# Output projection of a hybrid decoder layer: the second product of twelve pairs computed from HGRN2's half of y, among the attention's rest, with its sums kept in DRAM

## The chip, the cores and the metric

The kernel runs on one core of a Trainium2 chip. The metric is the device time of one execution in microseconds (us); the median of several runs is compared. The engines are TensorE (PE; its weight loads are listed apart as PEld), VectorE (DVE), ScalarE (ACT), GpSimd (POOL) and SyncE (SP), which issues every DMA of this kernel, in the order of its instructions. Each engine works through its own list in order, and waits where an instruction's operand isn't there yet.

## What is computed

The reference is one decoder layer over 4096 rows of width 1024, in float32. Cut to what matters:

```python
hn = _rmsnorm(x, mix_norm_w[layer])
proj = hn @ w_in[layer]                       # 1024 -> 4096 columns
...
y_attn = _head_rmsnorm(attn, ...) * silu(ag)  # 8 heads of 64, three dilated windows
y_hgrn = _head_rmsnorm(rec, ...) * silu(hg)   # 4 heads of 128, gated linear recurrence
mixed = jnp.concatenate([y_attn, y_hgrn], axis=-1)
x = x + mixed @ w_out[layer]
return _rmsnorm(x, final_norm_w)
```

The left half of `mixed` (512 columns) comes from the attention, the right half from the recurrence HGRN2. The kernel calls the two together `y` and keeps them in DRAM (`y_d`, 4096 x 1024).

## The kernel before, in words

**Stages.** First the attention's columns of the input projection, by 16 pairs of 128-row blocks. Then HGRN2's columns and its recurrence, head by head and pair by pair (`hgrn_pair`, L340), and beside it the attention: a generator, `attention()` (L624), from which `take` (L631) draws pieces between the pieces of HGRN2. When HGRN2's last pair is written, a part of the attention's eighth head is left, and `take(10 ** 9)` (L874) writes it all out: this is the attention's rest. Last comes the output projection with the residual and the final norm.

**The attention's rest.** It is the last part of head 7 at dilation 1: scores (`score`, L423/L424 on PE, L434 on DVE, L436 on ACT), transposes of the weights (`flip`, L446, with L449 on ACT and L450 on DVE), products with V (`weigh`, L458, whose V tiles `vh` are loaded at L531), and the sum of their two halves (`o`, L464 on ACT and L568 on DVE). After every eight blocks `finish` (L581) joins the three dilations: transposes (L603, L604), multiplications into the tile `pr` (L606 on DVE; the tile has one buffer), sums and norm on POOL (L609 to L618), and the store of 1024 rows of y (L619). There are four such stores for head 7. `summed_wo` (L968) is laid among it: it loads w_out (L974, four buffers `xr`), builds sums of its blocks on DVE (L982 to L989) and splits them (L858 on ACT, L859 on DVE).

**The output projection.** It is done by 16 pairs of row blocks, as a 2 x 2 by 2 x 2 block product with seven products in place of eight. Of a pair's y, `A11` is the attention's half of the first block, `A12` HGRN2's half of the first block, `A21` and `A22` the same of the second block; `B11` to `B22` are the 512 x 512 blocks of w_out, and S1 to S4 and T1 to T4 are sums of them. A product of 128 x 512 by 512 x 512 is called a half (`half`, L719): every operand is split into a rounded part (hi) and the rest (lo), and for each of four slices of 128 it takes three matmuls, hi·hi, hi·lo and lo·hi (L723, L724, L725), twelve in all. The first output block's left half is A11·B11 + A12·B21: `begin` (L919) does A11·B11 into a PSUM bank, copies it to `u2` (L927), does S4·B22 in between, adds A12·B21 into the first bank (L930) and adds the bank to the residual `xr` (L931). This A12·B21 is the pair's second product.

`load_y` (L876) loads the four quarters of a pair's y (L882, tile `vh`, three buffers), transposes each on PE in four pieces (L886) and makes the splits and sums on ACT, DVE and POOL (L170/L171, L893/L894, L901 to L909). `finish_pair` (L939) does the five other products, and `final_norm` (L958) the norm and the store. For each pair the loads of the next one are written ahead of its `finish_pair`.

**What sets the order.** The program is written in the order above, and a scheduler with its own model of the times then lays each engine's list. It moves instructions past one another where their operands allow it. Buffers limit it: tiles `raw` have three buffers, PSUM `proj` two, `hp1` and `po` one each, `att` four.

Of the kernel before, what the change touches and what calls it, by code (L numbers as in the profile page):

```python
# [49 lines left out]
def layer(ctx: ExitStack, tc: tile.TileContext, x, xT, xP, pos, w_in, w_out, nw, anw, hnw, lbraw, fnw,  # L50
# [7 lines left out]
    qk_d = [dram.tile([128, 4, S], F32, name=f"qk_d{p}") for p in range(4)]  # L58
    v_d = [dram.tile([S, 2, 128], F32, name=f"v_d{p}") for p in range(4)]
    xh_d = [dram.tile([4, 128, 1024], F32, name=f"xh_d{t}") for t in range(NB // 2)]  # L60
    sg_d = dram.tile([S, 512], F32, name="sg_d")
    y_d = dram.tile([S, D], F32, name="y_d")
    ml_d = dram.tile([NH, 2, 2, S], F32, name="ml_d")
# [655 lines left out]
    def half(ps, X, W, start=True):  # L719
        for k in range(4):  # L720
            c = slice(k * 128, (k + 1) * 128)
            (hi, lo), (whi, wlo) = X, W[k]
            T.matmul(ps, hi[:, c], whi, start=start and k == 0, stop=False, skip_group_check=not start)  # L723
            T.matmul(ps, hi[:, c], wlo, start=False, stop=False, skip_group_check=not start)  # L724
            T.matmul(ps, lo[:, c], whi, start=False, stop=(k == 3), skip_group_check=not start)  # L725
# [147 lines left out]
    dma(fnwt, fnw.partition_broadcast(128))  # L873
    take(10 ** 9)  # L874

    def load_y(t):  # L876

        a, X = {}, {}
# [9 lines left out]
        def split(name, src, eng, tags=None):  # L888
            if tags is None:
                X[name] = parts(split_tile(src, eng, xp, "xs", 5))  # L890
                return
            hi, lo = (tp.tile([128, 512], F32R, name=n, bufs=b) for n, b in tags)
            A.activation(hi, src, AF.Copy)  # L893
            eng.tensor_tensor(lo, src, hi.bitcast(F32), op=ALU.subtract)  # L894
            X[name] = hi, lo
# [6 lines left out]
        s2 = tp.tile([128, 512], F32, name="pot", bufs=2)  # L902
        V.tensor_tensor(s2, s1, a[0, 0], op=ALU.subtract)
        split("S2", s2, G, (("pt", 5), ("pt", 5)))
        split("A12", a[0, 1], V)
        split("S1", s1, G)
        V.tensor_tensor(a21, a[0, 0], a21, op=ALU.subtract)
        split("S3", a21, G, (("pt", 5), ("pt", 5)))
# [10 lines left out]
    def begin(t, X, third=True):  # L919

        xr = [fp.tile([128, D], F32, name="xr", bufs=4) for _ in range(2)]
        for i in range(2):
            dma(xr[i], x[(2 * t + i) * 128 : (2 * t + i + 1) * 128, :])
        pa = bank()
        half(pa, X["A11"], WO["B11"])
        u2 = fp.tile([128, 512], F32, name="u2", bufs=2)
        A.activation(u2, pa, AF.Copy)  # L927
        if third:
            third_product(X, xr)
        half(pa, X["A12"], WO["B21"], start=False)  # L930
        V.tensor_tensor(xr[0][:, c0], pa, xr[0][:, c0], op=ALU.add)  # L931
        return xr, u2

# [122 lines left out]
```

## Time and profile before

| | |
|---|---|
| median of 3 runs | 2739.09 us (2737.37 to 2740.02) |
| the profiled execution's own time | 2743.28 us |
| its span, first to last instruction | 2741.5 us |
| PE matmul busy | 2553.6 us (93%) |
| DVE busy | 2024.1 us (74%) |
| ACT busy | 1747.1 us (64%) |
| POOL busy | 1069.4 us (39%) |
| mean granted TensorE clock | 0.963 |

How to read it: times count from the span's start. A line such as `2507.41 0.39 PE L723 MATMUL att<-whi,xs ... x1` is the start, the duration, the engine, the line of the kernel, the operation, the tile written and the tiles read; a bracket behind it gives the idle time of the engine just before, and what ended it. In rows with groups, `x15 | 10.3, 687 | 4.8` means fifteen instructions, 10.3 us in all, 687 ns each, and 4.8 us of idle time ahead of them. Matmuls overlap, so that the time of a row of them is read from the difference of their starts. A wait reads: engine and line, what released it, us in total, times, the longest. PEclk is the share of full speed that TensorE's clock was granted.

### The profile page before, as it was taken

What the parts mean: (1) busy time and instruction counts of PE and PEld (TensorE: products, weight loads), DVE (VectorE), ACT (ScalarE), POOL (GpSimd) and SP (SyncE); (2) the same over time, 40 slices, a digit from 0 to 9 for tenths busy, and PEclk for the clock granted to TensorE, in tenths of its full rate; (3) what the DMA queues carried; (4) which work ended last, traced back from release to release, by engine and by line L of the source; (5) the groups of instructions that cost most, each with busy time, mean ns of one, the idle gap of its engine ahead of it and who ended that gap; (6) DMA issues with size and microseconds to landing.
All of it is one profiled execution on the core that took longest, in us unless ns stands there. A gap on an engine that the chain in (4) does not pass through costs nothing.

```text
span 2741.5 us, 51929 instructions
## 1 busy us (share of the span) xinstructions
PE 2553.6 (93%) x17138; PEld 2308.2 (84%) x17138; DVE 2024.1 (74%) x5310; ACT 1747.1 (64%) x4811; POOL 1069.4 (39%) x1012
## 2 busy tenths in 40 slices
PE   5899989999979999899999899999999998599998
PEld 4678867888879989799999799999899997488886
DVE  8787788777637788787787787776776877756665
ACT  7755565555548768768677678577686687434443
POOL 5455646665434464132231231331331421244443
PEclk8999999999979999999999899999999999699999
DMA  6854463444686775674874755855855743445453
GB/s 229 252 183 138 150 206 118 145 147 144 191 257 185 236 233 184 198 192 129 214 195 130 214 168 151 224 160 155 245 148 162 213 144 116 137 119 157 144 153 108
DMA packets 452192, 477.99 MB, mean 174 GB/s; under 512 B 119336, under 2 KB 334420, under 8 KB 451924
## 3 DMA queue, kind: packets, MB, share of 16 engines
q1 hardware_dynamic: 451924, 474.68, 58.6%
q8 instruction: 137, 2.24, 0.3%
q14 instruction: 131, 1.07, 0.1%
HBM read 348.16 MB, written 126.37 MB: 173 GB/s over the span
## 4 chain that ended last, share of the span: by engine, by line
PE 69%; DMA 10%; DVE 10%; ACT 4%; issue 3%; POOL 2%; SPq 1%; POOLq 0%; DVEq 0%; ACTq 0%
PE proj L199 19%; PE po L458 6%; PE m L725 6%; PE m L723 6%; PE m L724 6%; PE att L446 4%; PE att L723 3%; PE att L724 3%; PE att L725 3%; PE att L423 3%; PE att L424 3%; DMA y_d<-pr 1%; DMA raw<-x 1%; DVE pr L606 1%; DMA raw<-w_in 1%
## 5 line engine op out<-in xcount | busy, mean ns | idle before, releaser
L199 PE MATMUL proj<-xs,whi 128*128 128x256 f32 x2048 | 429.0, 294 | 21.6 <-ACT whi L161 12.1
L199 PE MATMUL proj<-whi,xs 128*128 128x256 f32 x2048 | 431.7, 293 | 4.2 <-DVE hz L306 4.2
L199 PEld LDWEIGHTS proj<-xs,whi 128*128 128x128 f32 x2048 | 331.2, 193 | 27.9 <-ACT whi L161 13.7
L199 PEld LDWEIGHTS proj<-whi,xs 128*128 128x128 f32 x2048 | 335.1, 193 | 5.9 <-DVE hz L306 4.5
L434 DVE CUSTOM_DVE_ANT_0 pt<-att,mask 128x256 f32<-128x256 f32 (+1 forms) x768 | 269.4, 388 | 75.8 <-PE att L424 73.7
L199 PE MATMUL proj<-xs,wlo 128*128 128x256 f32 x1024 | 300.5, 293 | 0.9 <-DVE wlo L162 0.9
L199 PE MATMUL proj<-wlo,xs 128*128 128x256 f32 x1024 | 300.0, 293 | 0.0
L450 DVE TENSOR_TENSOR pl<-att,ph 128x512 fp32r<-128x512 f32 (+1 forms) x384 | 237.7, 626 | 58.5 <-ACT ph L449 55.8
L436 ACT ACTIVATE pt<-pt,ml 128x256 f32<-128x256 f32 (+1 forms) x512 | 238.1, 467 | 55.3 <-DVE ml L434 54.2
L446 PE MATMUL att<-ident,pt 128*128 128x128 f32 x1368 | 228.3, 280 | 6.8 <-ACT pt L436 4.7
L449 ACT ACTIVATE ph<-att 128x512 fp32r<-128x512 f32 (+1 forms) x384 | 203.4, 542 | 47.4 <-PE po L458 28.6
L458 PE MATMUL po<-ph,vh 128*128 128x128 f32 (+1 forms) x856 | 212.4, 278 | 14.5 <-issue 10.1
L458 PE MATMUL po<-pl,vh 128*128 128x128 f32 (+1 forms) x856 | 207.3, 288 | 3.5 <-DVE pl L450 3.5
L199 PEld LDWEIGHTS proj<-xs,wlo 128*128 128x128 f32 x1024 | 197.3, 193 | 2.8 <-DVE wlo L162 1.3
L199 PEld LDWEIGHTS proj<-wlo,xs 128*128 128x128 f32 x1024 | 198.0, 193 | 1.2 <-issue 1.0
L458 PEld LDWEIGHTS po<-ph,vh 128*128 128x128 f32 x856 | 166.8, 195 | 19.4 <-issue 12.8
L446 PEld LDWEIGHTS att<-ident,pt 128*128 128x128 f32 x1368 | 162.3, 144 | 12.2 <-ACT pt L436 6.5
L458 PEld LDWEIGHTS po<-pl,vh 128*128 128x128 f32 x856 | 167.4, 196 | 5.2 <-DVE pl L450 4.7
L464 ACT ACTIVATE pot<-po 64x512 f32<-64x512 f32 (+1 forms) x256 | 124.4, 486 | 73.9 <-DVE o L568 37.9
L723 PE MATMUL m<-tw,ss 128*128 128x512 f32 x384 | 154.9, 404 | 15.2 <-ACT tw L170 7.4
L724 PE MATMUL m<-tw,ss 128*128 128x512 f32 x384 | 154.5, 402 | 4.1 <-DVE tw L171 4.1
L725 PE MATMUL m<-tw,ss 128*128 128x512 f32 x384 | 155.7, 406 | 0.0
(304 smaller groups left out, 7695.0 us busy)
## 6 DMA issues: line engine op xcount, KB each, us to landing
xs<-xh_d SPq DMA_DIRECT2D x192, 512.0 KB
xr<-xT SPq DMA_DIRECT2D x128, 256.0 KB
qk_d<-stk SPq DMA_DIRECT2D x128, 256.0 KB
xh_d<-xs SPq DMA_DIRECT2D x64, 512.0 KB
vh<-v_d SPq DMA_DIRECT2D x512, 64.0 KB
raw<-x SPq DMA_DIRECT2D x64, 256.0 KB
v_d<-hl SPq DMA_DIRECT2D x128, 128.0 KB
raw<-xP SPq DMA_DIRECT2D x64, 256.0 KB
```

Source lines behind the costliest of these rows:

```text
L199: m = T.matmul(o, l, r, start=first is None, stop=(k == KT - 1 and g == len(groups) - 1 and n == 2))
L423: T.matmul(o, q[:, j % 2 * 128 : (j % 2 + 1) * 128], cols(KH, *ks), start=True, stop=False)
L434: V.tensor_tensor_reduce(out=p_, in0=o, in1=mask[:, (1, 4, 16).index(d), 256 - 128 * nk : 256], scale=-0.125, scalar=3e38, op0=ALU.add, op ...
L436: A.activation(p_, p_, AF.Exp, scale=-1.0, bias=m, accum_out=l)
L446: T.transpose(ps[:, n * 128 : (n + 1) * 128], loc[u], ident)
L449: A.activation(ph[:, :w], ps[:, :w], AF.Copy)
L450: V.tensor_sub(pl[:, :w], ps[:, :w], ph[:, :w].bitcast(F32))
L458: T.matmul(po[:, 128 * c : 128 * (c + n)], v, rh, start=(s == 0), stop=(s == len(steps) - 1))
L464: A.activation(t[o : o + 64, c], po[64 - o : 128 - o, c], AF.Copy)
L723: T.matmul(ps, hi[:, c], whi, start=start and k == 0, stop=False, skip_group_check=not start)
L724: T.matmul(ps, hi[:, c], wlo, start=False, stop=False, skip_group_check=not start)
L725: T.matmul(ps, lo[:, c], whi, start=False, stop=(k == 3), skip_group_check=not start)
```

## The change

For the pairs 0 to 11 (`AHEAD = 12`) the second product is taken out of `begin` and computed earlier, in a loop of its own that is written behind `take(10 ** 9)` and ahead of the first `load_y`. For each such pair the loop loads HGRN2's half of the first block (`y_d[..., 512:1024]`, into a `raw` tile), transposes it on PE into `hp1`, splits it (hi on ACT, lo on DVE, into an `xs` tile), does the half with B21 into a `proj` bank, loads the left half of the same rows of x into another `raw` tile, adds the bank to it on DVE and stores the sum in DRAM (`p2_d[t]`, 256 KB).

In the output projection these pairs no longer split A12 and no longer do A12·B21. The residual tile of the first block is loaded in two parts, the stored sum for the left half and x for the right. All else of a pair is as before: the four loads and sixteen transposes of its y stay, since S4 needs A12 too. The pairs 12 to 15 are unchanged.

```diff
+    AHEAD = 12
+    p2_d = [dram.tile([128, 512], F32, name=f"p2_d{t}") for t in range(AHEAD)]
...
     take(10 ** 9)
 
+    for t in range(AHEAD):
+
+        yt = xp.tile([128, 512], F32, name="raw", bufs=3)
+        dma(yt, y_d[2 * t * 128 : (2 * t + 1) * 128, 512:1024])
+        pt_ = ps_h.tile([128, 512], F32, name="hp1")
+        for k in range(4):
+            c = slice(k * 128, (k + 1) * 128)
+            T.transpose(pt_[:, c], yt[:, c], ident)
+        a12 = parts(split_tile(pt_, V, xp, "xs", 5))
+        po2 = ps_p.tile([128, 512], F32, name="proj")
+        half(po2, a12, WO["B21"])
+        xt = xp.tile([128, 512], F32, name="raw", bufs=3)
+        dma(xt, x[2 * t * 128 : (2 * t + 1) * 128, 0:512])
+        V.tensor_tensor(xt, po2, xt, op=ALU.add)
+        dma(p2_d[t], xt)
...
-        split("A12", a[0, 1], V)
+        if t >= AHEAD:
+            split("A12", a[0, 1], V)
...
-            dma(xr[i], x[(2 * t + i) * 128 : (2 * t + i + 1) * 128, :])
+            rows = slice((2 * t + i) * 128, (2 * t + i + 1) * 128)
+            if i or t >= AHEAD:
+                dma(xr[i], x[rows, :])
+            else:
+                dma(xr[i][:, c0], p2_d[t])
+                dma(xr[i][:, c1], x[rows, c1])
...
-        half(pa, X["A12"], WO["B21"], start=False)
+        if t >= AHEAD:
+            half(pa, X["A12"], WO["B21"], start=False)
```

The scheduler lays the loop's instructions among those of the attention's rest; the lists that follow are its orders, before and in the changed kernel. The changed kernel's lines lie 2 further down to the loop, 18 further down in `load_y` and 25 further down from the end of `begin` on.

On DVE, ahead of head 7's second finish (the multiplications into `pr` that close each list), there stood before the sums of w_out's blocks (`xr`, `u2`), a piece of the norm (`nrr`) and the sum `o1`:

```order
L141 TENSOR_TENSOR nrr_29316<-nrr_29316,nrq_29319 128x8
L568 TENSOR_TENSOR o1_29516<-po_29563,pot_29577 64x256
L989 TENSOR_TENSOR xr_31984<-xr_31984,u2_31992 128x512
L982 TENSOR_TENSOR xr_32004<-xr_32004 128x512
L984 TENSOR_TENSOR u2_32013<-xr_32005,xr_32004 128x512
L987 TENSOR_TENSOR xr_32004<-xr_32005,xr_32004 128x512
L989 TENSOR_TENSOR xr_32005<-xr_32005,u2_32013 128x512
L606 TENSOR_TENSOR pr_29619<-att_29620,wt_29611 128x2x192
```

In the changed kernel the same place has adds of the new loop (L891, `proj` and x's `raw`) and a lo part (L173, from `hp1`):

```order
L142 TENSOR_SCALAR nrq_29331<-nrq_29331 128x8
L570 TENSOR_TENSOR o1_29528<-po_29575,pot_29586 64x256
L143 TENSOR_TENSOR nrr_29328<-nrr_29328,nrq_29331 128x8
L570 TENSOR_TENSOR o1_29528<-po_29575,pot_29589 64x256
L891 TENSOR_TENSOR raw_32035<-proj_32022,raw_32035 128x512
L173 TENSOR_TENSOR xs_32046<-hp1_32041,xs_32046 128x512
L891 TENSOR_TENSOR raw_32062<-proj_32049,raw_32062 128x512
L608 TENSOR_TENSOR pr_29631<-att_29632,wt_29623 128x2x192
```

The sums of w_out's blocks stand a little further up, and the adds of the turns 3 and 4 now stand directly ahead of the finish. By the twelfth turn, twelve such lo parts and eleven adds stand ahead of the first multiplication of the fourth finish.

On SP, before, the stretch from the last early load of w_out over finish's first and second store (`y_d` from `pr`), with the gate's load (`sgt`) and V's loads (`vh`):

```order
L974 DMA xr_32005<-w_out 128x1024
L531 DMA vh_29863<-v_d3_67 128x4x128
L619 DMA y_d_85<-pr_29287 128x8x64
L585 DMA sgt_29607<-sg_d_84 128x8x64
L531 DMA vh_29972<-v_d3_67 128x4x128
L531 DMA vh_30055<-v_d3_67 128x4x128
L619 DMA y_d_85<-pr_29619 128x8x64
```

In the changed kernel, the stretch around the first of these stores; `raw<-x` and `raw<-y_d` are the loop's loads and `p2_d` its stores:

```order
L890 DMA raw_32062<-x 128x512
L881 DMA raw_32066<-y_d_97 128x512
L892 DMA p2_d3_87<-raw_32035 128x512
L621 DMA y_d_97<-pr_29299 128x8x64
L587 DMA sgt_29619<-sg_d_96 128x8x64
L890 DMA raw_32089<-x 128x512
L881 DMA raw_32093<-y_d_97 128x512
L892 DMA p2_d4_88<-raw_32062 128x512
L890 DMA raw_32116<-x 128x512
L881 DMA raw_32120<-y_d_97 128x512
L892 DMA p2_d5_89<-raw_32089 128x512
L533 DMA vh_29984<-v_d3_67 128x4x128
```

Finish's first store stands behind the fourth stored sum, its second behind the seventh and its third behind the tenth; a turn puts a load of x, a load of y and a store on SP. As the three `raw` buffers fall, a load of x takes the buffer of the x two turns before, so it waits there until that turn's sum has landed.

## The prediction

> **What bounds the kernel now.** I read the page first, by its forty slices. A slice is 68.5 us; the digits are tenths of busy time, and in the third row tenths of TensorE's clock.
>
> ```profile
> PE   5899989999979999899999899999999998599998
> DVE  8787788777637788787787787776776877756665
> PEclk8999999999979999999999899999999999699999
> ```
>
> PE is full nearly everywhere, except in slice 34 (counted from 0; 2330 to 2398 us), and there its clock falls too. That is the rest of the attention, between HGRN2's last chunk and the output projection. I asked the windows for the two stages that the change touches: the rest, and sixteen pairs' steady part.
>
> ```profile
> core 0: us, PE busy (x) PEld busy (x) DVE busy (x) ACT busy (x) POOL busy (x), PEclk, DMA share, GB/s
> 2312.00:2323.00 11.00, 7.85 (x60) 6.69 (x58) 9.88 (x36) 6.72 (x23) 2.59 (x2) 1.00 0.18 49
> 2323.00:2337.00 14.00, 3.43 (x20) 2.08 (x18) 10.82 (x24) 3.84 (x12) 2.63 (x2) 0.68 0.72 244
> 2312.00:2388.00 76.00, 38.85 (x206) 31.43 (x205) 62.16 (x159) 36.85 (x100) 15.62 (x12) 0.67 0.43 135
> 2425.00:2700.00 275.00, 275.00 (x1319) 229.05 (x1318) 186.20 (x361) 116.59 (x283) 121.03 (x91) 1.00 0.52 153
> ```
>
> From 2425 on PE is busy all the time at full clock and DVE for 186.20 of 275 us: this stage is PE's. From 2312 to 2388 PE is busy for 38.85 of 76 us at a clock of 0.67, and DVE for 62.16: PE has 37 us to give, and DVE, with 13.84 us idle, is the fullest engine. What DVE's idle time waits for stands in the waits of this window:
>
> ```profile
> DVE o L568 <- ACT pot L464: 3.2, 2, 2.7
> DVE xr L982 <- DMA xr<-w_out: 2.9, 3, 1.9
> DVE pr L606 <- DMA y_d<-pr: 2.8, 2, 2.4
> DVE u L984 <- DMA xr<-w_out: 1.8, 2, 1.0
> ```
>
> These are a handful of waits of 1 to 2.7 us, for ScalarE and for transfers. So the rest is a DVE stream with a few holes, and its end releases the first pair.
>
> **The last stage: what is removed.** A half is twelve matmuls, and a pair has seven halves and sixteen transposes. In the timeline of PE one half runs from the first row below to the second, four transposes from the second to the third (0.44 us); the last two rows are the same place in two successive pairs.
>
> ```profile
> 2507.41 0.39 PE L723 MATMUL att<-whi,xs 128*128 128x512 f32 x1
> 2510.13 0.60 PE L886 MATMUL po<-ident,vh 128*128 128x128 f32 x4
> 2510.57 0.60 PE L886 MATMUL hp<-ident,vh 128*128 128x128 f32 x4
> ...
> 2519.62 0.39 PE L723 MATMUL att<-whi,xs 128*128 128x512 f32 x1
> 2540.56 0.39 PE L723 MATMUL att<-whi,xs 128*128 128x512 f32 x1
> ```
>
> The half takes 2.72 us and the pair 20.94, so a pair without its second product would take 18.22. DVE needs 186.20 / 275 x 20.94 = 14.2 us a pair, less the lo part that is dropped; ScalarE (8.9) and GpSimd (9.2) need less. PE stays the bound, so each pair gives back the whole half. What a pair needs of transfers stays the same: half of x is replaced by the stored sum of the same size, in one more issue on SP. What leaves DVE and ScalarE here (one split a pair) is worth nothing; both are hidden behind PE.
>
> The first pair is an exception. Its second product runs in a gap:
>
> ```profile
> 2386.90 0.79 PE L723 MATMUL att<-whi,xs 128*128 128x512 f32 x1 [3.44 <-DVE pr L606]
> 2392.18 0.63 PE L604 MATMUL att<-ident,o 128*128 128x128 f32 x2
> 2393.07 0.50 PE L723 MATMUL att<-whi,xs 128*128 128x512 f32 x1
> 2393.33 10.60 SPq L882 DMA_DIRECT2D vh<-y_d  x6
> 2396.79 0.60 PE L886 MATMUL hp<-ident,vh 128*128 128x128 f32 x4
> 2401.64 1.09 PE L886 MATMUL po<-ident,vh 128*128 128x128 f32 x4 [4.25 <-DMA vh<-y_d]
> ```
>
> It runs from 2393.07 on, beside a load of y issued at 2393.33 which the transposes at 2396.79 need, and the next load then keeps PE idle until 2401.64. Without the product PE would wait for the same loads. It gives between 0 and 2.85 us, and I take 0. So eleven pairs give 11 x 2.72 = 29.9 us.
>
> The first half of the stage (2386.90 to 2392.18) took 5.28 us, at half clock, behind a PE that had idled. In the changed order it stands right behind the twelfth moved product, so I take it at 2.72, which gives 2.56 us; the bounds are 0 and 2.56. It is on the path: the transposes behind it free the buffers for the loads that follow.
>
> **The rest: what is added.** Twelve times: two loads of 256 KB, four transposes, a split (hi on ScalarE, lo on DVE), a half, an add on DVE and a store of 256 KB. Durations come from the same forms in the last stage:
>
> ```profile
> L171 DVE TENSOR_TENSOR xs<-hp,xs 128x512 fp32r<-128x512 f32 x15 | 10.3, 687 | 4.8 <-ACT xs L170 4.8
> L931 DVE TENSOR_TENSOR xr<-att,xr 128x512 f32<-128x512 f32 x15 | 10.3, 690 | 2.6 <-PE att L725 1.3
> L170 ACT ACTIVATE xs<-hp 128x512 fp32r<-128x512 f32 x15 | 8.9, 593 | 10.5 <-PE att L725 10.4
> ```
>
> The order puts twelve lo parts and eleven adds on DVE ahead of the multiplications of the last finish: 12 x 0.687 + 11 x 0.690 = 15.8 us. DVE's idle time there is 13.84 us. If the new work filled all of it, the rest would grow by 2.0 us; if none, by 15.8. I take DVE at the share of its fullest attention window, 9.88 of 11 us or 0.90, because its holes are waits that new instructions fill only where they happen to be ready: (62.16 + 15.8) / 0.90 = 86.8 us in place of 76, **10.8 us more**. ScalarE's 12 x 0.593 = 7.1 us fit into its 39 idle us. PE's 12 x (2.72 + 0.44) = 38 us at full clock just about fit into its 37, and fit well if its own 38.85 us shrink as the clock comes back. The transfers (9.4 MB in 87 us, 108 GB/s) come on top of 135 GB/s; the window from 2323 shows 244.
>
> The queue SP gets 36 issues and their waits. An add must be done before its store is issued, and the load of x two turns later waits for that store to land; behind it on SP stand V's loads, finish's store of y and the loads of w_out. The nearest rows for a store's landing:
>
> ```profile
> 2436.71 0.58 SPq L966 DMA_DIRECT2D out<-xr  x1
> 2440.50 0.33 SPq L923 DMA_DIRECT2D xr<-x  x1
> ...
> 2318.97 1.63 DVE L386 SCALAR_TENSOR_TENSOR hgv<-hgv,hrr 128x128 f32<-128x128 f32 x2
> ...
> 2322.89 0.36 SPq L873 DMA_DIRECT2D fnwt<-fnw  x1
> 2323.30 1.85 SPq L974 DMA_DIRECT2D xr<-w_out  x4
> ...
> 2334.77 2.80 DMA y_d<-pr
> 2351.54 3.48 DMA y_d<-pr
> ...
> 2380.59 0.37 SPq L619 DMA_DIRECT2D y_d<-pr  x1
> ```
>
> The load at 2440.50 waited for the store of 2436.71: 3.79 us. With three issues of some 0.35 us a turn is about 4.8 us. The first add stands behind HGRN2's last multiplication on DVE, which ends at 2320.6, so the first store goes out near 2321.3. Finish's store of 2334.77 now stands behind the fourth: 2321.3 + 3 x 4.8 + 2.2 (the gamma and w_out issues that stand between) = 2337.9, 3.1 us late. Its store of 2380.59 stands behind the tenth, 9 x 4.8 = 43 us after the first, where 59.3 are there. So SP makes the first part late by 3.1 us and the later parts not; this lies inside the 10.8 and lifts its floor from 2.0 to about 3. [...]
>
> **The sum.** 10.8 - 29.9 - 2.6 = -21.7 us. The profiled execution took 2743.28 us (span 2741.5), 4.2 above the median of 2739.09. Its own time becomes 2721.6, and the median **2717.4 us**.
>
> **The rivals.**
> *The holes take everything.* PE regains its clock, its answers come sooner and DVE's holes are filled: the rest grows by 2 to 3 us. For it: 37 idle us on PE at a clock of 0.67. Against: the holes wait for ScalarE and transfers. 2739.09 + 2 - 32.5 = 2708.6. Chance 0.20.
> *PE stays cold half of the time.* The added halves come one by one behind waits. At the mean of 5.28 and 2.72 a half costs 4.0 us and its transposes 0.66, so PE needs 38.85 + 12 x 4.66 = 94.8 us in 76: the rest grows by 18.8, and the first half stays slow. 2739.09 + 18.8 - 29.9 = 2728.0. The clock's rows:
>
> ```profile
> 2403.23 0.78 PE L723 MATMUL att<-ph,qc 128*128 128x512 f32 x1
> 2406.36 0.44 PE L725 MATMUL att<-whi,xs 128*128 128x512 f32 x1
> ```
>
> After the idle 4.25 us the matmuls are slow from 2403.23 and fast from 2406.36, so a PE with work in hand is warm again within some 3 to 5 us. The Trainium skill (TensorE: Matmul & The Clock Gate, "What's actually happening") has the clock halve after an idle window of about 3.4 us and return after as long a busy one; the trace agrees, and by that rule gaps above 3.4 us between the moved halves would bring this rival about. Chance 0.14.
> *The last stage gives back half.* Something else takes over at a shorter pair, most likely SP, where the load of x waits for a store to land (3.79 us above, twice a pair). 2739.09 + 10.8 - 15.0 - 2.6 = 2732.3. Against: DVE needs 14.2 of 18.22 us. Chance 0.10.
> *The turns follow one another, and it is slower.* If only one turn were in flight on the three shared buffers, each would cost its whole chain:
>
> ```profile
> 2397.44 4.06 DMA vh<-y_d
> ```
>
> 4.06 (load) + 1.09 (transposes at half clock, 2401.64) + 0.59 + 0.69 + 5.28 + 0.69 + 3.48 (store) = 15.9 us. Nine turns are then 143 us where 59.3 are there: the rest grows by 84, and the time is 2739.09 + 84 - 29.9 = 2793. It is slower from 9 T - 59.3 > 29.9 on, T = 9.9 us a turn. Against: x has two of the three buffers, which halves T to 7.9 (9 x 7.9 - 59.3 = 12 us, close to what I took). Chance 0.06.
> That the work isn't moved at all is excluded by the order: all twelve products stand ahead of the first pair's first half, among the instructions of the attention's rest.
>
> **How the numbers follow.** My forecast has 0.50. A measurement of this kernel can tell about 0.2%, 5.5 us, from no change. Forecast and first rival are faster by far more; the second and third reach into the 5.5 us at their upper ends (0.06 together); slower is the fourth, 0.06. The range 2705 to 2732 goes from just under the first rival (where the first pair's product gives its 2.85 us too) to the third.
>
> **What would show it.** Right: twelve pairs with a period near 18.2 us and four of 20.9; the first pair's first half about 11 us later than 2386.90 and 2.7 us long; DVE's share from 2312 on near 0.9, the granted clock there above 0.9. Wrong: halves of 5 us among the attention's rest; SP waiting on stores of the sums while finish's store stands behind them; gaps on PE between 2425 and the end.

## The result and the profile after

The changed kernel takes 2724.61 us (median of 4 runs, 2719.2 to 2726.4), against 2738.23 us of the kernel before beside it (2735.35 to 2740.02). The ratio is 0.9938, 95% interval 0.992 to 0.9955: faster by 0.6%, some 17 us by the ratio (12 to 22 by its interval), where 21.7 were predicted. The two medians lie 13.6 us apart; where an interval stands with a difference below, the difference goes by the ratio. The changed kernel's profiled execution took 2725.64 us (span 2723.9), which against 2743.28 (2741.5) is 17.6 us less.

The page of the changed kernel, two rows of its forty slices:

```profile
PE   5899989999979999999999899999899999889998
PEclk8999999999979999999999899999999998999999
```

Slice 34, which stood at 5 for PE and 6 for its clock, now reads 8 and 9. The windows of the changed kernel, the two stretches of before and, as a third, the rest from HGRN2's last matmul to the first S4 (its own ends, 103.70 us apart):

```profile
core 0: us, PE busy (x) PEld busy (x) DVE busy (x) ACT busy (x) POOL busy (x), PEclk, DMA share, GB/s
2312.00:2388.00 76.00, 65.35 (x355) 53.09 (x356) 61.35 (x164) 36.82 (x99) 13.44 (x11) 0.91 0.65 204
2425.00:2700.00 275.00, 272.57 (x1308) 225.76 (x1307) 206.91 (x378) 114.56 (x287) 133.96 (x102) 1.00 0.53 159
2309.20:2412.90 103.70, 81.78 (x444) 65.99 (x442) 81.58 (x201) 51.71 (x133) 23.73 (x19) 0.91 0.65 206
```

The same stretch of the kernel before, between its own ends:

```profile
2310.30:2403.20 92.90, 50.61 (x256) 41.19 (x256) 70.63 (x175) 43.97 (x116) 23.17 (x18) 0.69 0.43 136
```

PE took the added work at nearly full clock (0.91 for 0.69). DVE's busy time in the rest rose by 11.0 us and the rest by 10.8: DVE's idle time is 22.1 us, and was 22.3. In the last stage PE is no longer busy without a break. Its waits for y, in the changed kernel's waits of PE from 2425 to 2712 (the only other row is 1.6 us ahead of the very last product, which the kernel before has as well):

```profile
PE proj L904 <- DMA vh<-y_d: 2.3, 3, 0.9
```

The first half of the last stage and the first S4, in the changed kernel's timeline of PE (the first row ends the twelfth moved half):

```profile
2397.77 0.40 PE L727 MATMUL proj<-whi,xs 128*128 128x512 f32 x1
2398.01 0.60 PE L904 MATMUL hp<-ident,vh 128*128 128x128 f32 x4
2398.36 0.48 PE L725 MATMUL att<-whi,xs 128*128 128x512 f32 x1
2401.07 0.39 PE L727 MATMUL att<-whi,xs 128*128 128x512 f32 x1
2401.29 0.60 PE L904 MATMUL proj<-ident,vh 128*128 128x128 f32 x4
...
2411.28 1.09 PE L904 MATMUL po<-ident,vh 128*128 128x128 f32 x4 [3.95 <-ACT qc L911]
...
2412.87 0.78 PE L725 MATMUL att<-ph,qc 128*128 128x512 f32 x1
```

That half starts at 2398.36, 11.5 us later than before, and takes 2.93 us in place of 5.28. So the 17.6 us come about like this (starts in the timelines of PE, us):

| stretch | before | changed | difference |
|---|---|---|---|
| start to HGRN2's last matmul | 2310.3 | 2309.2 | -1.1 |
| from there to the first half (A11) | 76.6 | 89.2 | +12.6 |
| from there to the first S4 | 16.3 | 14.5 | -1.8 |
| from there to PE's end | 328.3 | 301.0 | -27.3 |

**Where the rest got longer.** The starts of finish's four stores were 2334.77, 2351.54, 2380.59 and 2409.39; they are now 2339.57, 2360.65, 2389.72 and 2416.54. From HGRN2's last matmul to the second store it was 41.2 us and is 51.5; from the second to the third 29.1 and 29.1. Nearly the whole delay lies ahead of the second store, where eight of the twelve turns run. A part of what happens there stands in the changed kernel's timeline of DVE, from the first to the last of the four small steps of finish's first norm:

```profile
2331.64 0.15 DVE L140 TENSOR_TENSOR nrq<-nrr 128x8 f32<-128x8 f32 x1
2332.08 0.69 DVE L891 TENSOR_TENSOR raw<-proj,raw 128x512 f32<-128x512 f32 x1 [0.29 <-PE proj L727]
2332.80 0.43 DVE L570 TENSOR_TENSOR o<-po,pot 64x256 f32<-64x256 f32 x1
2333.26 0.69 DVE L1009 TENSOR_TENSOR u<-xr 128x512 f32<-128x512 f32 x1
2333.87 0.68 DVE L1012 TENSOR_TENSOR xr<-xr 128x512 f32<-128x512 f32 x1
2334.47 0.16 DVE L141 TENSOR_TENSOR nrq<-nrq,nrm 128x8 f32<-128x8 f32 x1
2334.66 0.69 DVE L173 TENSOR_TENSOR xs<-hp,xs 128x512 fp32r<-128x512 f32 x1
2335.27 0.68 DVE L1014 TENSOR_TENSOR xr<-xr,u 128x512 f32<-128x512 f32 x1
2335.87 0.17 DVE L142 TENSOR_SCALAR nrq<-nrq 128x8 f32<-128x8 f32 x1
2335.94 0.41 DVE L570 TENSOR_TENSOR o<-po,pot 64x256 f32<-64x256 f32 x1
2336.28 0.15 DVE L143 TENSOR_TENSOR nrr<-nrr,nrq 128x8 f32<-128x8 f32 x1
```

The first and the last of the same four steps in the kernel before:

```profile
2329.71 0.16 DVE L138 TENSOR_TENSOR nrq<-nrr 128x8 f32<-128x8 f32 x1
...
2331.73 0.16 DVE L141 TENSOR_TENSOR nrr<-nrr,nrq 128x8 f32<-128x8 f32 x1
```

A turn's add and lo part and the sums of w_out's blocks stand between steps that need 0.15 to 0.17 us each: from the start of the first to the end of the last it takes 4.8 us, where it took 2.2. GpSimd multiplies by `nrr` next, and only then is the store of y ready. In the changed kernel's timelines of POOL and of SP:

```profile
2336.57 1.04 POOL L619 TENSOR_TENSOR pr<-pr,nrr 128x512 f32<-128x512 f32 x1 [14.15 <-DMA p_d<-raw]
2337.69 1.27 POOL L620 TENSOR_TENSOR pr<-pr,sgt 128x512 f32<-128x512 f32 x1
```

```profile
2339.57 0.38 SPq L621 DMA_DIRECT2D y_d<-pr  x1
```

`nrr` is done at 2336.43, GpSimd takes it at 2336.57 (the transfer that the bracket names is no operand of it) and is through with `pr` at 2338.96; SP issues the store 0.6 us later.

DVE is not the only engine on this path. The profile also gives the chain of work that ended last, each step followed back to what released it. In the changed kernel's chain from 2330 to 2362, the shares by line and three of its pieces (a piece is start, duration, what; the sums' tiles `p2_d` are listed as `p_d`):

```profile
by line: DMA y_d<-pr 26.0%; PE proj L727 12.5%; DMA p_d<-raw 10.8%; PE proj L726 10.6%; PE proj L725 9.2%; PE po L460 7.7%; PE hp L885 6.0%; PE att L448 5.5%; PE att L425 4.0%; PE att L426 3.0%; PE att L605 2.0%; issue 1.9%; DVE pr L608 1.8
2339.57 4.71 DMA y_d<-pr
2356.79 3.47 DMA p_d<-raw
2360.28 0.33 SPq L890
```

This chain runs through the landings of the stores and through the moved halves on PE (L725 to L727, 32%), and hardly through DVE. The first store of y took 4.71 us to land, where it took 2.80 before, and the second finish's multiplications into `pr` wait for that. The second store stands on SP behind a load of x that waited 3.47 us for a stored sum to land; since GpSimd is through with `pr` only at 2360.38, this costs 0.3 us. So DVE's, PE's and SP's ways to these stores end within 0.6 us of one another, and the timelines alone don't say which of them sets the rest.

### The profile page after: what moved, and what is told of

Read it like the earlier page. It is cut to its first block, busy times and chain, and to the rows that moved or that the text cites. A ratio compares the mean times of both kernels' runs of the same rounds, so it can differ in the third digit from the quotient of the medians.

```text
span 2723.9 us, 52124 instructions
## 1 busy us (share of the span) xinstructions
PE 2559.8 (94%) x17186; PEld 2310.5 (85%) x17186; DVE 2042.7 (75%) x5322; ACT 1743.4 (64%) x4811; POOL 1066.0 (39%) x1012
## 5 line engine op out<-in xcount | busy, mean ns | idle before, releaser
L201 PE MATMUL proj<-xs,whi 128*128 128x256 f32 x2048 | 432.1, 296 | 20.9 <-ACT whi L163 12.3
L201 PEld LDWEIGHTS proj<-xs,whi 128*128 128x128 f32 x2048 | 333.9, 194 | 27.2 <-ACT whi L163 13.7
L725 PE MATMUL m<-tw,ss 128*128 128x512 f32 x384 | 155.0, 404 | 16.9 <-ACT tw L172 6.6
L727 PE MATMUL m<-tw,ss 128*128 128x512 f32 x384 | 155.9, 406 | 0.0
```

Of the source, the lines that this page charges most:

```text
L201: m = T.matmul(o, l, r, start=first is None, stop=(k == KT - 1 and g == len(groups) - 1 and n == 2))
```

## The experiments

Three theories of the rest's 11 us stood against each other. **A**: DVE; what the turns add to its list is paid for. **B**: SP and the transfers; waits on the queue, and landings that are longer. **C**: PE; the added halves in its one list hold up the attention's transposes and scores. Ratios are to the kernel before. Since the program ahead of the rest came out between 2299.8 and 2321.0 us in these executions, the profiles are compared from HGRN2's last matmul on: to the first S4 ("rest"), from there to PE's end ("last stage").

| kernel | rest | DVE busy in it | last stage | both | ratio (interval) |
|---|---|---|---|---|---|
| before | 92.9 | 70.6 | 328.3 | 421.2 | |
| changed | 103.7 | 81.6 | 301.0 | 404.7 | 0.9938 (0.992 to 0.9955) |
| again | 104.2 | 81.9 | 300.5 | 404.7 | 0.9937 (0.9921 to 0.9954) |
| last_only | 91.4 | 72.1 | 303.1 | 394.5 | 0.9918 (0.9902 to 0.9934) |
| rest_only | 103.6 | 83.7 | 328.4 | 432.0 | 1.0037 (1.0022 to 1.0053) |
| dve_free | 107.9 | 75.1 | 300.8 | 408.7 | 0.9950 (0.9927 to 0.9972) |
| no_dma | 122.8 | 84.7 | 301.7 | 424.5 | 1.0008 (0.9996 to 1.002) |
| quarter | 110.5 | 85.1 | 302.3 | 412.8 | 0.9968 (0.9955 to 0.9981) |
| dve_twice | 112.8 | 89.2 | 304.6 | 417.4 | 0.9978 (0.9964 to 0.9993) |
| ahead16 | 118.5 | 88.0 | 295.8 | 414.3 | 0.9962 (0.9948 to 0.9976) |
| thin | 94.7 | 74.4 | 305.2 | 399.9 | 0.9941 (0.9918 to 0.9965) |
| pool_lo | 97.6 | 79.6 | 306.0 | 403.6 | 0.9947 (0.9927 to 0.9966) |
| before_pool_lo | 87.6 | 68.0 | 328.1 | 415.7 | 0.9988 (0.9974 to 1.0002) |
| yrawt | 101.4 | 80.6 | 300.3 | 401.6 | 0.9935 (0.9918 to 0.9953) |

**The changed kernel once more (again).**

> The changed kernel once more, as the yardstick of this chip. Every theory: 2724 us, about 14 to 17 us under the kernel before.

2721.73 us, 0.9937. Rest and last stage repeat within 0.5 us, though HGRN2's end came 6.8 us earlier than in the other execution.

**The two halves of the change apart: last_only and rest_only.**

> The moved loop is left out altogether, and with it the second product of the pairs 0 to 11, which is in no output row then; x is loaded whole. This is the change's gain in the last stage alone. Theory of the prediction (eleven halves of 2.72 us count, the first pair's is hidden behind the loads of y, the first half stays at half clock): 29.9 us under the kernel before, 2708. Rival (a pair of 18.2 us runs into waits for its own loads of y, whatever the stored sums do): about 27 us under it, 2711, with the same gaps on PE as in the changed kernel. If the first pair's product counted too: 32.6 under it, 2705.6.

```diff
-    for t in range(AHEAD):
...
-        V.tensor_tensor(xt, po2, xt, op=ALU.add)
-        dma(p2_d[t], xt)
...
-            if i or t >= AHEAD:
-                dma(xr[i], x[rows, :])
-            else:
-                dma(xr[i][:, c0], p2_d[t])
-                dma(xr[i][:, c1], x[rows, c1])
+            dma(xr[i], x[rows, :])
```

> The loop stays with its loads and stores, and the last stage is that of the kernel before, with its own second products and x loaded whole (the stored sums are used by nobody). This is the change's cost in the rest alone. Theory of the prediction: 10.8 us more in the rest, less 2.6 for a first half at full clock: 8 us above the kernel before, 2746. If the two parts don't add up, this run and last_only differ from the changed kernel by more than 3 us in their sum, and something that they share was missed.

```diff
-        if t >= AHEAD:
-            split("A12", a[0, 1], V)
+        split("A12", a[0, 1], V)
...
-        if t >= AHEAD:
-            half(pa, X["A12"], WO["B21"], start=False)
+        half(pa, X["A12"], WO["B21"], start=False)
```

(rest_only also loads x whole in the last stage, so that the stored sums are read by nobody.) last_only took 2716.96 us, 22.5 less than before (interval 18 to 27): less than the 29.9 of the prediction's theory, and at the rival's 27 only by the end of its interval. rest_only took 2750.39, 10.1 more (6 to 14.5; 8 were expected). Together -12.4, where the whole change gives -17. That is 4.6 us apart, over the 3 us that were set as the sign of something missed, but the intervals are too wide to tell. In the profiles the two parts add up: last_only is 26.7 us shorter (rest -1.5, last stage -25.2), rest_only 10.8 longer (+10.7 and +0.1), -15.9 together where the change has -16.5. The shorter last stage brings its own waits. In last_only's waits of PE, without a loop or a stored sum:

```profile
PE proj L888 <- DMA vh<-y_d: 3.6, 3, 2.2
```

These waits come from the shorter pairs, not from the stored sums.

**Work taken off DVE, first try (dve_free).**

> The loop's lo part and its add are taken off DVE: ScalarE copies the transposes and the product out of PSUM (two plain copies a turn, some 1.2 us), GpSimd subtracts and adds (2.6 us a turn). Theory A, that the rest grew because DVE, its fullest engine, got 15.8 us more: most of the 10 us go, 2714 to 2717. Theory B, that it grew because the loads, the stores and their waits on SP made finish's stores late: no change, 2722 to 2726. Theory C, that the halves stand in PE's order ahead of the attention's matmuls: no change or, with two more steps in each turn, some us more, 2724 to 2730.

```diff
-        a12 = parts(split_tile(pt_, V, xp, "xs", 5))
+        cp = tp.tile([128, 512], F32R, name="qc", bufs=2).bitcast(F32)
+        A.activation(cp, pt_, AF.Copy)
+        a12 = parts(split_tile(cp, G, xp, "xs", 5))
...
-        V.tensor_tensor(xt, po2, xt, op=ALU.add)
+        so = tp.tile([128, 512], F32R, name="qc", bufs=2).bitcast(F32)
+        A.activation(so, po2, AF.Copy)
+        G.tensor_tensor(xt, so, xt, op=ALU.add)
```

The rest got longer by 4 us more, not shorter, and the time of 2729.45 us lies where C had it (2724 to 2730). But the move put 24 instructions on GpSimd, which makes `pr` ready for its store. In dve_free's timeline of POOL, finish's two last steps with a lo part between them and an add ahead:

```profile
2338.57 1.54 POOL L895 TENSOR_TENSOR raw<-qc,raw 128x512 f32<-128x512 f32 x1 [7.23 <-ACT qc L894]
2340.28 1.04 POOL L619 TENSOR_TENSOR pr<-pr,nrr 128x512 f32<-128x512 f32 x1 [0.17 <-DVE nrr L143]
2341.28 1.26 POOL L173 TENSOR_TENSOR xs<-qc,xs 128x512 fp32r<-128x512 f32 x1
2342.49 1.27 POOL L620 TENSOR_TENSOR pr<-pr,sgt 128x512 f32<-128x512 f32 x1
```

And its waits of DVE in the rest:

```profile
DVE pr L608 <- DMA y_d<-pr: 13.5, 2, 7.4
```

13.5 us of waiting for finish's stores, for 2.6 in the changed kernel: the kernel moved the load into the same chain one engine further. So it tells nothing of A, and nothing for C.

**Transfers out (no_dma), matmuls out (quarter), DVE's work doubled (dve_twice).**

> The loop keeps its loads of y, its transposes, halves and adds, but the add takes the norm's gain tile in place of x and nothing is stored; the last stage loads x in the same two parts, so the second product of the pairs 0 to 11 is in no output. 24 of the loop's 36 issues on SP and 6.3 of its 9.4 MB go. The measure is the stretch from HGRN2's last matmul to the first S4: 92.9 us before, 103.7 changed. Theory A, DVE's added 15.8 us set the stretch: nothing they do goes, 103 to 105 us, 17 us faster than before as the change is. Theory B, the waits on SP and the longer landings set it: 96 to 100 us, 21 to 25 us faster than before. Theory C, PE's added halves in its one list, which hold up the transposes of finish and the scores: as theory A, 103 to 105 us.

```diff
-        dma(xt, x[2 * t * 128 : (2 * t + 1) * 128, 0:512])
-        V.tensor_tensor(xt, po2, xt, op=ALU.add)
-        dma(p2_d[t], xt)
+        V.tensor_tensor(xt, po2, fnwt[:, 0:512], op=ALU.add)
...
-                dma(xr[i][:, c0], p2_d[t])
+                dma(xr[i][:, c0], x[rows, c0])
```

> The loop's half does three of its twelve matmuls, so that the sums it stores lack most of the second product; loads, transposes, splits, adds and stores stay. PE has 12 x 9 x 0.227 = 24.5 us less to do in the rest. Theory C, PE's list: the stretch from HGRN2's last matmul to the first S4 falls from 103.7 to 94 to 98 us, and the kernel is 23 to 27 us faster than before. Theories A (DVE) and B (SP and transfers): the stretch stays at 101 to 105 us, 17 to 20 us faster than before.

```diff
-        half(po2, a12, WO["B21"])
+        T.matmul(po2, a12[0][:, 0:128], WO["B21"][0][0], start=True, stop=False)
+        T.matmul(po2, a12[0][:, 0:128], WO["B21"][0][1], start=False, stop=False)
+        T.matmul(po2, a12[1][:, 0:128], WO["B21"][0][0], start=False, stop=True)
```

> Each turn of the loop computes its lo part twice on DVE: 12 x 0.69 = 8.3 us more on DVE, nothing else more. Theory A, DVE is the rest's bound: the stretch from HGRN2's last matmul to the first S4 grows from 103.7 to 111 to 113 us, and the kernel is only 8 to 10 us faster than before. Theories B and C: DVE still has 16 us of idle time in that window, and the stretch grows by 0 to 3 us, to 104 to 107 us; 14 to 17 us faster than before.

```diff
         a12 = parts(split_tile(pt_, V, xp, "xs", 5))
+        V.tensor_tensor(a12[1], pt_, a12[0].bitcast(F32), op=ALU.subtract)
```

no_dma was none of what the theories expected: 122.8 us of rest, and as slow as the kernel before. Without the loop's loads and stores the scheduler laid the turns otherwise; only four run ahead of the second store, and the last six after the attention's last transposes, one after another. The transposes of the last three, in its timeline of PE:

```profile
2406.78 0.60 PE L885 MATMUL hp<-ident,raw 128*128 128x128 f32 x4
2411.23 0.60 PE L885 MATMUL hp<-ident,raw 128*128 128x128 f32 x4
2415.65 0.60 PE L885 MATMUL hp<-ident,raw 128*128 128x128 f32 x4
```

A turn that runs alone costs 4.4 us, more than the 2.7 us that it saves. The run can't judge B by its time; what it shows is that a turn must lie among other work.

quarter's rest was 110.5 us, longer than with all matmuls and than any theory had it. Its window of the rest:

```profile
2315.30:2425.80 110.50, 68.28 (x336) 53.73 (x335) 85.06 (x204) 52.77 (x134) 23.06 (x19) 0.72 0.61 193
```

PE is busy for 68.28 us in place of 81.78, at a clock of 0.72, and the rest is 6.8 us longer: fewer matmuls did not give the rest back, as C in its plain form has it. But here too the turns moved (eleven start ahead of the second store), so this run alone doesn't exclude C.

dve_twice's window of the rest:

```profile
2299.80:2412.60 112.80, 85.08 (x439) 66.95 (x438) 89.16 (x212) 51.45 (x131) 21.97 (x18) 0.90 0.58 187
```

The rest grew to 112.8 us, A's 111 to 113, with DVE 7.6 us busier; B and C had 104 to 107. The time (2733.43 us, 6 us under before, 2 to 10 by the interval) is below A's 8 to 10, since the last stage was 3.6 us longer as well, and far from the 14 to 17 of B and C. One thing goes along with it: the doubled lo part also stands in each turn's own chain, ahead of its half, and this run doesn't separate the two. Idle time of DVE: 23.6 us. With 22.3 before, 22.1 and 22.3 in the changed kernel and 19.9 in rest_only, A took a new form: the rest is DVE's busy time and some 22 us that new work doesn't fill. The 22 is no constant, though: most other runs have 18.0 to 25.4 us, and dve_free, no_dma and ahead16 30.5 to 38.1.

**Sixteen pairs (ahead16).**

> All sixteen pairs in place of twelve. In the last stage four more halves go, 4 x 2.72 = 10.9 us less. In the rest, if each turn adds the same (theories A, B and C alike, 10.8 / 12 = 0.9 us a turn), the stretch from HGRN2's last matmul to the first S4 grows by 3.6 us to 107 us, and the kernel is 24 us faster than before. If the twelve turns already fill what PE and DVE had to give, each further turn costs PE its whole 3.2 us: 116 us, and the kernel is as fast as with twelve, 15 to 18 us faster than before.

```diff
-    AHEAD = 12
+    AHEAD = 16
```

Four more turns cost 14.8 us of rest, 3.7 each: near the second case (116 us), and worse in all, 10 us under before (7 to 14) where 15 to 18 were expected. DVE's idle time is 30.5 us, since the last four turns run nearly alone, as in no_dma. The last stage gave only 5.2 us for four halves, where 10.9 were expected.

**DVE's work thinned (thin).**

> Each turn's lo part and its add cover 128 of the 512 columns (the matmuls of hi by lo all read that one slice, and three quarters of a stored sum are x alone); every load, transpose, matmul, issue and store stays, and the turns keep their places in PE's order within a few rows. DVE's 128x128 subtraction took 0.29 us in the changed kernel, so DVE has 12 x 2 x 0.40 = 9.5 us less. Theory A in its new form, the stretch from HGRN2's last matmul to the first S4 is DVE's busy time there plus 22 us that don't change (70.9 of 92.9 us before, 81.8 of 103.7 changed, 89.2 of 112.8 with the lo part twice): 103.7 falls to 93 to 97 us, and the kernel is 24 to 28 us faster than before. Theories B (SP and transfers) and C (PE's list): the stretch stays at 102 to 105 us, 17 us faster than before.

```diff
-        a12 = parts(split_tile(pt_, V, xp, "xs", 5))
+        a12 = parts(xp.tile([128, 1024], F32R, name="xs", bufs=5))
+        A.activation(a12[0], pt_, AF.Copy)
+        V.tensor_tensor(a12[1][:, 0:128], pt_[:, 0:128], a12[0].bitcast(F32)[:, 0:128], op=ALU.subtract)
...
+            T.matmul(po2, a12[1][:, 0:128], whi, start=False, stop=k == 3)
...
-        V.tensor_tensor(xt, po2, xt, op=ALU.add)
+        V.tensor_tensor(xt[:, 0:128], po2[:, 0:128], xt[:, 0:128], op=ALU.add)
```

Its window of the rest:

```profile
2321.00:2415.70 94.70, 75.24 (x428) 60.86 (x426) 74.37 (x202) 49.97 (x130) 21.62 (x18) 0.95 0.67 217
```

All transfers, issues and matmuls are there, 202 instructions on DVE for 201, and the rest is 94.7 us: A's 93 to 97, not the 102 to 105 of B and C. DVE is 7.2 us less busy and idle for 20.3. The time is not what A expected, though: 0.9941 is 16 us (10 to 22) under before, not 24 to 28, and that is what B and C expected. Of the rest's 9 us, 4.2 come back as a longer last stage, because what stood ahead of the first S4 now partly stands behind it: five groups of transposes precede it in place of nine, and two groups of the second pair come at 2416.68 and 2417.53, after the S4 at 2415.67, which itself stands behind 3.5 us of waits for loads of y. So part of the 9 us is order. To the start of the first half the rest is only 3.1 us shorter (86.1 for 89.2), and from HGRN2's last matmul to PE's end 4.8 us are left (399.9 for 404.7), which a measurement can't tell from nothing. Once DVE is through earlier, the first pair waits for its loads. So work added to the turns on DVE costs its full time in the rest and shows in the kernel's time (dve_twice); that work taken off DVE comes back in full is not shown.

**The same relief by another road (pool_lo, before_pool_lo).**

> The changed kernel with the lo parts of T1 to T4, sixteen in all, on GpSimd in place of DVE; nothing is left out. In the rest DVE loses 12 x 0.77 + 4 x 0.68 = 11.9 us; GpSimd, busy for 25 of the 104 us there, gains 16 x 1.29 = 20.6 us. Theory A: the stretch from HGRN2's last matmul to the first S4 falls from 103.7 to 92 to 97 us, and the kernel is 24 to 29 us faster than before. Theories B and C: the stretch stays at 103 to 106 us (a lo part among finish's steps on GpSimd can hold a store by up to 2.6 us), 15 to 17 us faster than before.

```diff
-    def split_wo(raw, hi, lo):
+    def split_wo(raw, hi, lo, eng=V):
...
-        V.tensor_sub(lo, raw, hi.bitcast(F32))
+        eng.tensor_tensor(lo, raw, hi.bitcast(F32), op=ALU.subtract)
...
-                WO[name][k] = split_wo(src, t[:, c0], t[:, c1])
+                WO[name][k] = split_wo(src, t[:, c0], t[:, c1], G)
```

> The same move of sixteen lo parts to GpSimd in the kernel before. Theory A: the rest is DVE's there too, and the stretch from HGRN2's last matmul to the first S4 falls from 92.9 to 82 to 87 us, 6 to 11 us faster than before. If DVE became the bound only with the turns' work: 91 to 95 us, no difference.

Sixteen subtractions left DVE, 11.9 us by their rows. pool_lo's window of the rest:

```profile
2310.30:2407.90 97.60, 77.42 (x435) 62.57 (x434) 79.62 (x183) 50.38 (x129) 43.62 (x33) 0.94 0.68 215
```

The rests fell by 6.1 and 5.3 us and end just above A's 92 to 97 and 82 to 87, while DVE's busy time fell by 2.0 and 2.6 us only (its idle time is 18.0 and 19.6 us, so here most of the fall is idle time, which A's form doesn't have). What else left DVE's list was eaten up by longer instructions. The groups of DVE in pool_lo from 2362.8 to 2407.9:

```profile
L861 DVE TENSOR_TENSOR pl<-xr,ph 128x512 fp32r<-128x512 f32 x4 | 6.0, 1515 | 0.0
L891 DVE TENSOR_TENSOR raw<-proj,raw 128x512 f32<-128x512 f32 x5 | 3.4, 687 | 1.4 <-PE proj L727 1.3
L1014 DVE TENSOR_TENSOR xr<-xr,u 128x512 f32<-128x512 f32 x2 | 2.5, 1250 | 0.0
```

The same three in the changed kernel, from 2360.7 to 2412.9:

```profile
L891 DVE TENSOR_TENSOR raw<-proj,raw 128x512 f32<-128x512 f32 x5 | 3.4, 681 | 1.3 <-PE proj L727 1.3
L861 DVE TENSOR_TENSOR pl<-xr,ph 128x512 fp32r<-128x512 f32 x4 | 2.6, 684 | 0.0
L1014 DVE TENSOR_TENSOR xr<-xr,u 128x512 f32<-128x512 f32 x2 | 1.4, 682 | 0.0
```

The two groups with both operands in SBUF take 1250 to 1515 ns in place of 682 to 684 beside a busy GpSimd, the one that reads a PSUM bank (`proj`) 687 for 681. Both kernels gain little: 0.9947, 15 us under before (9 to 20), which is what B and C expected and no better than the changed kernel, and 0.9988 (0.9974 to 1.0002). In pool_lo, too, the first half starts only 1.5 us earlier (87.7 for 89.2). Whether the rest was DVE's before the change as well stays open: before_pool_lo's 87.6 us to the first S4 lie nearer to A's 82 to 87 than to the other case's 91 to 95, but the first half starts 2.0 us later than before (78.6 for 76.6), and the time shows no difference.

**A fourth buffer for y in the last stage (yrawt).**

> The changed kernel with a fourth buffer for y in the last stage: from pair 1 on, the load of a pair's fourth quarter goes to a raw tile, which nothing else uses there; nothing is left out. The measure is the stretch from the first S4 to PE's end: 328.3 us before, 301.0 and 300.5 in two executions of the changed kernel, with 2.3 and 1.9 us of waits for loads of y (before: none). If a load of y comes late because it waits for the tile that the transposes free, the waits go and the stretch falls to 298 to 299 us; the kernel is 18 to 20 us faster than before. If the transfers themselves are late (the landings are longer beside the stores of the output), the waits stay, with a stretch of 300 to 301.5 us and 17 us faster than before.

```diff
-            yt = tp.tile([128, 512], F32, name="vh", bufs=3)
+            yt = xp.tile([128, 512], F32, name="raw", bufs=3) if t and (i, j) == (0, 1) else tp.tile([128, 512], F32, name="vh", bufs=3)
```

The waits for loads of y are gone; yrawt's only row in the waits of PE from 2425 to 2712:

```profile
PE att L725 <- DVE xr L978: 0.7, 4, 0.2
```

But the last stage is 300.3 us, not 298 to 299, and the time, 0.9935, is the changed kernel's. A late buffer was the cause of those waits, as expected; taking them away brought only 0.7 us of their 2.3 (301.0 before it, 300.5 in the other execution). Two parts of the rest can be named: the 0.7 us of new waits for DVE in the row above, and one group of four transposes (0.44 us) that now stands behind the first S4 in place of ahead of it. The others are not settled.

No kernel here computes the layer and is measurably faster than the changed one.

## Why the prediction was right, and where it wasn't

The time, 2724.61 us, lies in the range of 2705 to 2732 and on the side given 0.88; it is 7.2 us above the 2717.4. By steps:

**The rest, 10.8 us predicted, +12.6 to the first half.** That work added to DVE lengthens it was right: the run with the lo part doubled shows it, in the rest and in the time. That DVE alone sets it is not shown. The two runs that relieve it shorten the stretch to the first S4 as A has it, or nearly, but part of that is order, and their times are those of B and C; the runs without the transfers and with fewer matmuls had their turns laid otherwise; and the chain ahead of the second store runs through PE and the landings.

The size was right by luck. The step "I take DVE at the share of its fullest attention window, 9.88 of 11 us or 0.90, because its holes are waits that new instructions fill only where they happen to be ready" failed: none of the idle time was filled on balance. DVE's share went from 0.76 to 0.79 (81.58 of 103.70) and not to 0.90, and its idle time stayed at 22 us. What kept the sum right is that DVE's busy time grew by 11.0 us where twelve lo parts and twelve adds make 12 x 0.685 + 12 x 0.687 = 16.5 by their rows. There are two reasons. The rows overlap: behind one another such instructions start 0.60 us apart though each lasts 0.68 (2333.26, 2333.87 and 2334.47 above), so that the durations of all rows together grew by 13.7 us and the busy time by 11.0. And other instructions became shorter. In the groups of DVE the sixteen sums of w_out's blocks took 13.7 us before and 11.6 after, sixteen lo parts of theirs 12.3 and 11.8, and HGRN2's last multiplications 2.2 and 1.1. Those read SBUF alone, the kind that pool_lo lengthened; that they ran beside GpSimd less often now was not tried by itself.

**SP.** The first store was predicted 3.1 us late by SP and is 4.8 late, of which SP's list has 0.6 (ready at 2338.96, issued at 2339.57). The norm's small steps on DVE have 2.6 of it (4.8 us for 2.2), and their first one starts 1.9 us later. "The later parts not" was wrong as well: the second is 9.1 late, and the longer landing of the first has 1.9 of that. SP waiting on a sum's store with finish's store behind it, a sign that the prediction gave for being wrong, is there at the second store and costs 0.3 us.

**The last stage, -29.9 predicted, -27.3.** Of a pair's seven products `begin` does three and `finish_pair` four. Eleven halves left the stage, as the prediction counted, and 27.3 / 11 is 2.48 us each in place of 2.72. Pair 0's product was taken as worth nothing, and that was right: it stood ahead of the first S4, and PE now waits there instead (next paragraph). The period was to be 18.22 us; the pairs 3 to 11 take 18.29 on average, 164.6 in all where it was 188.0, or 2.60 us a half. Single periods, counted from S4 to S4, depend on where the products stand in PE's list (17.11, 18.15 and 19.26 in turn): pair 1's second product stood in the period of pair 0, which gave 2.77 (17.95 to 15.18), so that the next period had none to lose (17.65 to 17.05), and the one after gave only 0.52, with ten transposes more in it than one pair has and 0.9 us of waiting for y. Only the sum of the first twelve is a fair number: 244.5 us before, 217.2 after. The 2.3 us of waits for y are nearly all of the missing 2.6 in this execution: without them the stage would be 29.6 us shorter. The prediction had no term for them: it took a pair's transfers as unchanged, and last_only shows that the shorter pair alone brings such waits. Yet taking them away, in yrawt, did not bring the 2.3 us back.

**The first half, -2.6 predicted, -1.8.** It is 2.93 us long, 2.35 less. Behind it pair 0's product is gone too, 2.85 us, but PE now waits 3.13 us for DVE and 3.95 for ScalarE ahead of the first S4, where it had waited 4.25 for a load.

**The sum.** 12.6 - 1.8 - 27.3 is -16.5 us, and 1.1 us came from ahead of the rest; that the start of the rest moves by several us from one execution to the next is seen in all runs. The terms that were mis-sized are the last stage, by 2.6 us, the rest, by 1.8, and the first half, by 0.8.

**The rivals.** The holes take everything: no, on balance the holes took nothing. PE cold half of the time: parts of four of the twelve moved halves ran at half clock, but the clock of the rest was 0.91 and the first half took 2.93 us. The last stage gives back half: it gave back 2.6 of 29.9 us. The turns follow one another: not with twelve, whose turns start 5.0 to 12.1 us apart among other work; but in ahead16 and no_dma the last turns did so, at 4.4 us and more a turn.

## What to carry to other kernels

An idle share on the fullest engine of a stage need not be room. Here the holes were waits of a chain of dependent steps that runs through that engine and others, and work added to its list lengthened the stage by its full busy time; small steps of the chain waited between large instructions. Count what a moved piece adds to the engine that sets the stage it moves into, against what it frees on the engine that sets the stage it leaves: here about 0.9 us for 2.3 a pair. And a piece that fills a stage pays only while there is other work beside it: the last four of sixteen turns cost 3.7 us each and gave 1.3.

## What the runs showed of the hardware

In pool_lo, GpSimd instructions that read SBUF held up DVE instructions whose two operands are both in SBUF: 684 ns became 1515 on average over four (the subtraction for B22), 682 became 1250 over two, and GpSimd's own subtractions for w_out took 1431 and 1440 ns where three others of their shape in the same window took 1279 to 1285. One of the two of 1250 ns, 1.16 us long, starts at 2386.69 beside a GpSimd subtraction that runs from 2385.58 for 1.72 us. DVE instructions with one operand in PSUM did not change (681 and 687 ns). The Trainium skill (SBUF — State Buffer, "Who interferes with whom") has the two engines share one port pair, which one holds for the whole of an instruction; the measured groups agree. So moving 11.9 us of SBUF work from DVE's list to GpSimd took only about 2 us off DVE's busy time.

TensorE's clock fell after a shorter gap than I had expected. In the changed kernel's timeline of PE, within the eleventh moved half:

```profile
2380.82 0.40 PE L726 MATMUL proj<-wlo,xs 128*128 128x512 f32 x1
2383.68 0.68 PE L727 MATMUL proj<-whi,xs 128*128 128x512 f32 x1 [2.46 <-DVE xs L173]
2384.15 0.63 PE L725 MATMUL proj<-whi,xs 128*128 128x512 f32 x1
2384.58 0.63 PE L726 MATMUL proj<-wlo,xs 128*128 128x512 f32 x1
```

Behind an idle time of 2.46 us the matmuls start 0.43 us apart, and are fast again from 2387.4 on, 3.7 us later. The Trainium skill (TensorE: Matmul & The Clock Gate, "What's actually happening") gives one idle window of about 3.4 us for the fall, which the prediction's rival took over as gaps above 3.4 us; the return agrees with it, the fall here came sooner.
